# A hybrid RWKV-7, latent and stick-breaking attention layer: two issuing queues for the DMAs, and less filler around the inverse

## The chip, the cores and the metric

The kernel runs on one core of a Trainium2 chip. The metric is the device time of one execution in microseconds (us), as the median of the runs shown. Five engines of the core work side by side and wait for each other by semaphores: TensorE (PE in the profile; its weight loads are PEld), VectorE (DVE), ScalarE (ACT), GpSimd (POOL) and SyncE (SP), which here only issues DMAs. A DMA can be issued from SyncE or from ScalarE; an issue is an instruction in the engine's own order and stands in the trace as SPq or ACTq.

## The reference

One layer over 1024 tokens of width 1024, in float32. A normalized copy of x goes through one wide projection, its columns feed three token mixers side by side, their outputs are joined, projected and added to x, and a SwiGLU network follows.

```
h = rms_norm(x, attn_norm_g) @ w_in
r, k, v, wd, ad, gd = split(token_shift(h[..., :RW_COLS], mu))
c_q, c_kv, k_rope, sb_q, sb_k, sb_v = split(h[..., RW_COLS:])
y_rw  = rwkv7_time_mix(r, k, v, wd, ad, gd, ...)      # 8 heads of 64, a scan over time:
#   sa = S @ a_t;  S = S * w_t + sa b_t^T + v_t k_t^T;  y_t = S @ r_t
y_mla = latent attention of rms_norm(c_q) @ w_uq, rms_norm(c_kv) @ w_ukv   # 4 heads, rotary, softmax
y_sb  = stick-breaking attention of sb_q, sb_k, sb_v                        # 4 heads
x = x + concat(y_rw, y_mla, y_sb) @ w_o
hn = rms_norm(x, ffn_norm_g)
x = x + (silu(hn @ w_gate) * (hn @ w_up)) @ w_down    # 2816 hidden
```

## The kernel before

**Products.** A float32 product is made of three TensorE products (`mm3`) of a high and a low part of each operand: `wsplit` copies the high part on ScalarE and subtracts on GpSimd (or another engine), so every weight takes a load, an activation and a subtraction. `load_split` loads a block of 128 columns of `w_in` (512 KB) into one of three buffers `wr` and splits it. Products go to banks of PSUM that are given out by tag ("cu", "cy", "av", "b" and others); a tag has a fixed number of buffers, and a new user waits until the last one's copy out is done.

**Stages.** First the projection of r, k, v of the RWKV heads (column blocks in pairs of heads, `pr` 0 to 3, and halves of 512 tokens), and the operands of the scan in chunks of 64 tokens. For a chunk and head these are a strictly lower triangular 64 x 64 matrix (`d_a`), the matrices in `d_ch` (Lt, BK and RX side by side, 1 MB for each of 16 chunks) and the values (`d_v`). All go to DRAM and come back in another layout. In `s3` VectorE masks a bank into the tile `gs` (two buffers), and three DMAs store parts of it: the transposed part (`lt_out`), a block of `d_rx` (the RX part of `d_ch`) and the block for `d_a`.

**The inverse.** For each of the 128 pairs of chunk and head the triangular matrix is inverted. The two 32 x 32 diagonal blocks of all pairs are loaded into `TT` by 16 DMAs, and VectorE and GpSimd build their inverses in `XB` step by step (`inverse_steps`). `inverse_out` stores the first block's transpose to `d_x1t` and both blocks to `d_rx` (16 stores), `merge_loads` loads what `merge_a` needs (`x11` from `d_x1t`, `x22` back from `d_rx`), and the off-diagonal block is made by two rounds of 32 x 32 products, `merge_a` (bank `mga`, copied to `mgr`) and `merge_b` (bank `mgb`, copied to `mgm`), each for two groups of four heads, and stored to `d_rx`.

**The chain.** Sixteen `chain_step`s follow each other over the chunks. A step's operands come by `chain_loads`, issued on ScalarE: `CT` (the chunk's 1 MB of `d_ch`) and `SU` (state and values), with two buffers each. The products are y, u, s and y again, with copies on ScalarE and a sum on VectorE between them. `y_rows` normalizes rows, and after 8 and 16 chunks `rw_finish` scales them on GpSimd, transposes them (`yt`), multiplies by the gate (`gg`) and writes the mixed rows.

**Background.** A generator (`background`) yields everything else that is ready: the latent projections (`ip_ckv`, `uq`, `ukv`), the q and k heads (`tqq`, `tqk`), the stick-breaking inputs (`ip_sk`, stored by `sb_half` as a high and a low tile `sth` and `stl`), and then the attention, heads 0 to 3 stick-breaking and 4 to 7 with softmax (scores, weights `wt` split to `wth` and `wtl`, products `av`). `fill(n)` takes from it until its pieces come to n of the kernel's own estimated us. The program places such calls between the steps of the inverse (FILL_INV), after its stores (FILL_OUT), after each merge (FILL_MG), before the chain (FILL_END) and within it (FILL).

**Order.** Written order isn't issued order: a scheduler with a timeline of its own puts each engine's instructions in a row when the kernel is built, and an engine then works through its row without passing anything. After the chain comes the output projection `wo`, then the network with `hid`, `up` and `fd`.

Of the kernel before, what the change touches and what calls it, by code (L numbers as in the profile page):

```python
# [10 lines left out]
F32 = mybir.dt.float32  # L11
# [47 lines left out]
def trunk_kernel(ctx: ExitStack, tc: tile.TileContext, a: dict, out: bass.AP):  # L59
# [22 lines left out]
    def raw(ap):  # L82
        return ap.bitcast(F32)

    LNEXP = "natural_log_exp_and_others"

    def use_ln_exp():
# [34 lines left out]
    d_v = dr.tile([2, T, RWW // 2], F32, name="d_v")  # L122
    d_pl = dr.tile([RWW, NCH], F32, name="d_pl")
    d_x1t = dr.tile([RWH * NCH, L // 2, L // 2], F32, name="d_x1t")
    d_bv = dr.tile([4, P, T], F32, name="d_bv")
    d_sg = dr.tile([2, P, T], F32, name="d_sg")
    d_sq = dr.tile([2, 2 * P, T], F32, name="d_sq")
# [57 lines left out]
    def load_split(src_ap, c, name, eng=None):  # L185
        n = src_ap.shape[1] * c
        r, h, l = wtiles(name, n)
        nc.sync.dma_start(r.rearrange("p (a b) -> p a b", b=c), src_ap)
        wsplit(r, h, l, eng)
        return h.rearrange("p (a b) -> p a b", b=c), l.rearrange("p (a b) -> p a b", b=c)  # L190

# [135 lines left out]
    def sb_half(dst, blk, nm, hf, o):  # L327

        ts_ = slice(hf * HALF, (hf + 1) * HALF)
        h, l = stg(f"sth{nm}{blk}{hf}"), stg(f"stl{nm}{blk}{hf}")  # L330
        nc.scalar.activation(h, o, AF.Copy)
        tt(nc.vector, l, o, raw(h), ALU.subtract)
        for i, t_ in enumerate((h, l)):
            nc.sync.dma_start(dst[i, blk * P : (blk + 1) * P, ts_], raw(t_))

    def sb_block(c0, dst, blk, nm):
        for hf, o in enumerate(inproj_cols(c0 + blk * P, f"{nm}{blk}")):
# [3 lines left out]
    with tc.tile_pool(name="qa", bufs=1, reuse_waits="tile") as qa:  # L341
# [139 lines left out]
        def s3(pr, hf):  # L481
# [4 lines left out]
            for q in range(2):  # L486
                c0 = hf * 8 + q * 4

                ogs = [bank(f"g{n}_{e}{q}") for e in range(2)]
                for c in range(4):  # L490
                    for e, og in enumerate(ogs):
                        rows_ = slice(e * 64, e * 64 + 64)
                        nc.tensor.matmul(og[:, c * P : (c + 1) * P], BK[rows_, q * 4 + c].rearrange("p a t -> p (a t)"),
                                         AR[rows_, q * 4 + c].rearrange("p a t -> p (a t)"), start=True, stop=True)
                for e, og in enumerate(ogs):
                    gs = qa.tile([P, 4, P], F32, tag="gs", bufs=2, name=f"gs{n}_{e}{q}")
                    tt(nc.vector, gs, og.rearrange("p (c t) -> p c t", c=4), gmask[:, None, :].to_broadcast([P, 4, P]), ALU.mult)
                    lt_out(slice(c0, c0 + 4), R2[1 - e], 2 * pr + e, gs[64:128])
                    nc.sync.dma_start(d_rx[c0 : c0 + 4, R2[e], 2 * pr + e, :].rearrange("c s t -> s c t"), gs[0:64, :, 64:128])
                    nc.sync.dma_start(d_a[2 * pr + e, c0 : c0 + 4].rearrange("c s t -> s c t"), gs[0:64, :, 0:64])  # L500

            ov = bank(f"vt{n}")
            for j in range(4):
# [127 lines left out]
    nc.gpsimd.memset(XB, 0.0)  # L631
    for b in range(2):
        for h in range(RWH):
            nc.sync.dma_start(TT[h * NCH : (h + 1) * NCH, b], d_a[h, :, b * HB : (b + 1) * HB, b * HB : (b + 1) * HB])
        nc.gpsimd.memset(XB[:, b].rearrange("p a b -> p (a b)")[:, 0 : HB * HB : HB + 1], 1.0)

    def inverse_steps(j0, j1):
# [18 lines left out]
    def inverse_out():  # L656
        X1 = TT[:, 0]
        nc.vector.tensor_copy(X1, XB[:, 0].rearrange("p a b -> p b a"))
        nc.sync.dma_start(d_x1t.rearrange("n a b -> n (a b)"), X1.rearrange("p a b -> p (a b)"))
        for b in range(2):  # L660
            r0, r1 = b * HB, (b + 1) * HB
            for h in range(RWH):
                nc.sync.dma_start(d_rx[:, xrow(h) + r0 : xrow(h) + r1, h, r0:r1], XB[h * NCH : (h + 1) * NCH, b])
# [7 lines left out]
    def hb_rows(tag, h):  # L671
        return hb[tag, h // 4][h % 4 * HB : (h % 4 + 1) * HB]

    def merge_loads():
        for h in range(RWH):
            nc.sync.dma_start(hb_rows("x11", h), d_x1t[h * NCH : (h + 1) * NCH].rearrange("n a b -> a n b"))
            nc.sync.dma_start(hb_rows("x22", h), d_rx[:, xrow(h) + HB : xrow(h) + L, h, HB:L].rearrange("n a b -> a n b"))

    def merge_a(g):

        o = bank(f"mga{g}", "cu")
        for c in range(NCH):
            for k in range(4):
                ks = slice(k * HB, (k + 1) * HB)
                nc.tensor.matmul(o[ks, c * HB : (c + 1) * HB], hb["a21", g][ks, c, :], hb["x11", g][ks, c, :], start=True, stop=True)
        nc.scalar.activation(hb["mgr", g].rearrange("p c t -> p (c t)"), o, AF.Copy)

    def merge_b(g):
        o = bank(f"mgb{g}", "av")
        for c in range(NCH):  # L690
            for k in range(4):
                ks = slice(k * HB, (k + 1) * HB)
                nc.tensor.matmul(o[ks, c * HB : (c + 1) * HB], hb["mgr", g][ks, c, :], hb["x22", g][ks, c, :], start=True, stop=True)
        nc.scalar.activation(hb["mgm", g].rearrange("p c t -> p (c t)"), o, AF.Copy)
        for h in range(4 * g, 4 * g + 4):
            nc.scalar.dma_start(d_rx[:, xrow(h) : xrow(h) + HB, h, HB:L].rearrange("n a b -> a n b"), hb_rows("mgm", h))


    uqh = qb.tile([P, 2, 384], F32R, name="uqh")
# [395 lines left out]
            yield p_()  # L1095
        fin()

    FILL_INV, FILL_OUT, FILL_MG, FILL_END, FILL = 6, 34, 4, 18, 1.9
    LATE_PER_ATT = 1
    SB_POOL, MLA_POOL = (1, 3, 5), (1, 3, 5)  # L1100

# [6 lines left out]
    for h in range(RWH):  # L1108
        nc.sync.dma_start(hb_rows("a21", h), d_a[h, :, 0:HB, HB:L].rearrange("c s t -> s c t"))
    inverse_out()  # L1110
    merge_loads()
    fill(FILL_OUT)
    for g in range(2):
        merge_a(g)
        fill(FILL_MG)
    for g in range(2):
        merge_b(g)
        fill(FILL_MG)
    fill(FILL_END)
    qi_cm.__exit__(None, None, None)  # L1120

# [535 lines left out]
```

## Time and profile before

| what | value |
|---|---|
| time, median of 3 runs | 1446.31 us (1444.57 to 1447.97) |
| profiled execution, time | 1447.62 us |
| profiled execution, span | 1445.4 us |
| TensorE busy | 1341.4 us, 93% |
| VectorE busy | 921.7 us, 64% |
| GpSimd busy | 689.1 us, 48% |
| ScalarE busy | 652.5 us, 45% |
| DMA | 201.29 MB, mean 139 GB/s |

Busy times are those of one profiled execution and don't add up, since the engines work side by side. The idle share of the engine that is busiest says how much a better order could bring at all (104 us of TensorE here, over all stages), but where it stands idle, and for whom, has to be read from single stretches. The profile gives the clock that TensorE was granted in tenths of full speed; it is 9 or more in all of the 40 slices but two, at about 397 to 470 us, with 8.

### The profile page before, as it was taken

The page shows a single profiled execution, that of the slowest core. Times are in us where ns is not written, and L with a number is a line of the kernel's source. Part 1 is how long each engine was busy: PE and PEld are TensorE (multiplying, and loading weights), DVE is VectorE, ACT ScalarE, POOL GpSimd, SP SyncE. Part 2 cuts the span into 40 slices and gives each one's busy share as a digit, 9 for nine tenths or more (in the row PEclk, how much of TensorE's full clock was granted, in tenths as well). Part 3 has the DMA queues.
Part 4 walks back from the last instruction along what each step waited for, and adds up shares of the span by engine and source line. Part 5 has one row for each costly group of instructions (what it writes and reads, how often), then busy time and mean ns, then how long its engine had stood idle before and what let it go on. Part 6 is the DMA issues. An engine that isn't in the chain of part 4 may idle for free.

```text
span 1445.4 us, 21569 instructions
## 1 busy us (share of the span) xinstructions
PE 1341.4 (93%) x7717; PEld 1100.2 (76%) x7717; DVE 921.7 (64%) x1316; ACT 652.5 (45%) x1306; POOL 689.1 (48%) x664
## 2 busy tenths in 40 slices
PE   6999999898868988997998899999999999999998
PEld 6777778777656776886787688888888888778786
DVE  6566575377248899675137966656655565797755
ACT  6645345223447786886424433333333333434342
POOL 3233342376243335231605776666666666445443
PEclk9999999999988999999999999999999999999999
DMA  7226555785779652742432432322333217843242
GB/s 228 50 63 160 141 144 146 193 142 111 193 207 268 179 172 66 227 136 88 157 134 90 133 113 102 109 93 98 109 110 110 80 60 274 329 160 102 80 139 73
DMA packets 229444, 201.29 MB, mean 139 GB/s; under 512 B 92077, under 2 KB 180442, under 8 KB 227418
## 3 DMA queue, kind: packets, MB, share of 16 engines
q1 hardware_dynamic: 216362, 175.28, 41.0%
q10 hardware_dynamic: 12976, 24.65, 5.5%
q8 instruction: 61, 1.00, 0.3%
q14 instruction: 45, 0.37, 0.1%
HBM read 131.95 MB, written 67.93 MB: 138 GB/s over the span
## 4 chain that ended last, share of the span: by engine, by line
PE 58%; DVE 14%; DMA 7%; ACT 6%; SPq 5%; issue 5%; POOL 3%; ACTq 0%; DVEq 0%; POOLq 0%
PE fd L205 4%; PE fd L206 3%; PE fd L204 3%; PE wo L205 2%; PE wo L206 2%; PE wo L204 2%; PE wt L916 1%; DVE C L987 1%; PE y L1155 1%; DMA d_a<-gs 1%; DVE l_w L91 1%; DVE gs L91 1%; SPq L447 1%; DVE wd L91 1%; POOL XB L91 1%
## 5 line engine op out<-in xcount | busy, mean ns | idle before, releaser
L91 POOL TENSOR_TENSOR l_h<-hr,h_h 128x512 fp32r<-128x512 f32 x77 | 106.7, 1387 | 108.5 <-ACT h_h L1315 100.8
L205 PE MATMUL fd<-l_w,h_h 128*128 128x512 f32 x308 | 120.0, 394 | 8.9 <-DVE l_w L91 8.8
L91 DVE TENSOR_TENSOR l_w<-wd,h_w 128x512 fp32r<-128x512 f32 x77 | 90.3, 1181 | 49.4 <-ACT h_w L1315 49.3
L206 PE MATMUL fd<-h_w,l_h 128*128 128x512 f32 x308 | 118.9, 391 | 0.0
L1315 ACT ACTIVATE h_h<-hr 128x512 fp32r<-128x512 f32 x77 | 48.7, 633 | 136.3 <-PE fd L205 89.4
L204 PE MATMUL fd<-h_w,h_h 128*128 128x512 f32 x308 | 84.1, 392 | 0.0
L91 POOL TENSOR_TENSOR l_ffn_w_up<-rffn_w_up,h_ffn_w_up 128x512 fp32r<-128x512 f32 x33 | 47.1, 1428 | 67.0 <-ACT h_ffn_w_up L1315 61.3
L205 PEld LDWEIGHTS fd<-l_w,h_h 128*128 128x128 f32 x308 | 58.1, 189 | 24.0 <-DVE l_w L91 12.1
L204 PEld LDWEIGHTS fd<-h_w,h_h 128*128 128x128 f32 x308 | 58.4, 190 | 12.2
L206 PEld LDWEIGHTS fd<-h_w,l_h 128*128 128x128 f32 x308 | 58.1, 189 | 11.9
L91 POOL TENSOR_TENSOR hid<-hid,up 128x512 f32<-128x512 f32 x44 | 62.7, 1425 | 9.2 <-DVE up L91 9.2
L91 POOL TENSOR_TENSOR BD<-BK,plt 64x512 f32<-64x512 f32 (+1 forms) x24 | 35.9, 1497 | 55.1 <-DVE BK L91 41.8
L91 DVE TENSOR_TENSOR wtl<-wt,wth 128x512 fp32r<-128x512 f32 (+2 forms) x112 | 54.2, 491 | 12.3 <-ACT wth L921 8.2
L91 POOL TENSOR_TENSOR l_ffn_w_gate<-rffn_w_gate,h_ffn_w_gate 128x512 fp32r<-128x512 f32 x33 | 48.0, 1457 | 22.8 <-ACT h_ffn_w_gate L1315 22.8
L921 ACT ACTIVATE wth<-wt 128x512 fp32r<-128x512 f32 (+2 forms) x112 | 48.1, 445 | 16.8 <-PE wt L916 6.1
L1496 ACT ACTIVATE hid<-hid 128x512 f32<-128x512 f32 x44 | 27.7, 632 | 61.1 <-DVE hid L91 61.1
L205 PE MATMUL wo<-wol,mix 128*128 128x512 f32 x128 | 50.3, 394 | 0.0
L206 PE MATMUL wo<-woh,mix 128*128 128x512 f32 x128 | 50.2, 393 | 0.0
L204 PE MATMUL wo<-woh,mix 128*128 128x512 f32 x128 | 49.7, 397 | 0.0
L1315 ACT ACTIVATE h_ffn_w_gate<-rffn_w_gate 128x512 fp32r<-128x512 f32 x33 | 20.8, 631 | 61.2 <-PE P4up L205 21.5
L1315 ACT ACTIVATE h_w<-wd 128x512 fp32r<-128x512 f32 x77 | 47.5, 617 | 0.5 <-PE fd L206 0.4
L91 DVE TENSOR_TENSOR gs<-g,gmask 128x512 f32<-128x512 f32 x32 | 21.3, 684 | 38.8 <-DMA d_a<-gs 38.8
(569 smaller groups left out, 4409.1 us busy)
## 6 DMA issues: line engine op xcount, KB each, us to landing
CT<-d_ch ACTq DMA_DIRECT2D x15, 1024.0 KB
hr<-d_h SPq DMA_DIRECT2D x14, 1024.0 KB
rffn_w_gate<-in_ffn_w_gate_dram SPq DMA_DIRECT2D x11, 1024.0 KB
rffn_w_up<-in_ffn_w_up_dram SPq DMA_DIRECT2D x11, 1024.0 KB
d_h<-up SPq DMA_DIRECT2D x44, 256.0 KB
d_h<-hid SPq DMA_DIRECT2D x33, 256.0 KB
wd<-in_ffn_w_down_dram SPq DMA_DIRECT2D x8, 1024.0 KB
hr<-d_h SPq DMA_DIRECT2D x7, 768.0 KB
```

What stands on the lines that cost most here:

```text
L91: eng.tensor_tensor(o, x, y, op=op)
L204: nc.tensor.matmul(o, lh, rh, start=first, stop=False)
L205: nc.tensor.matmul(o, lh, rl, start=False, stop=False)
L206: nc.tensor.matmul(o, ll, rh, start=False, stop=last)
L447: nc.sync.dma_start(d_lt[chunks, rows, h, o].rearrange("c s t -> s c t"), src[:, :, i])
L916: nc.tensor.transpose(o[:, (sb * 2 + i) * P : (sb * 2 + i + 1) * P], W[i][:, (2 * g + sb) * P : (2 * g + sb + 1) * P], ident)
L921: nc.scalar.activation(wh[:, lo:hi], o[:, lo:hi], AF.Copy)
L987: nc.vector.tensor_tensor_scan(C[:, k1 - 1 : last : -1], st[:, k1 - 1 : last : -1], zero_c.to_broadcast([P, k1 - k0]), 1.0 if k1 == n else ...
L1155: nc.tensor.matmul(yo[:, ps[h]], Lt[:, h, :], S[:, ps[h]], start=h == 0, stop=True, skip_group_check=True)
L1315: nc.scalar.activation(hv, src, AF.Copy)
L1496: nc.scalar.activation(hid[f][hf], hid[f][hf], AF.Silu)
```

## The change

The constants for the filler become smaller (34 to 12, 4 to 2, 18 to 10), and FILL_MG is taken once between the merges instead of four times. `QUEUES` is a pair of SyncE and ScalarE. ScalarE issues the loads of `load_split`, the low tiles of `sb_half`, half of the 16 loads of the diagonal blocks, and half of the merged stores; the `d_a` store goes ahead of the two others of its tile, for the last pair of heads on ScalarE. The inverse's second block gets a DRAM buffer of its own (`d_x22`), stored by ScalarE, and the loads of `x11` and `x22` are issued before the 16 stores to `d_rx`, the former on SyncE, the latter on ScalarE. The merges' banks get a tag each in turn. No arithmetic is changed.

```diff
+    QUEUES = (nc.sync, nc.scalar)
...
+    d_x22 = dr.tile([RWH * NCH, L // 2, L // 2], F32, name="d_x22")
...
     def load_split(src_ap, c, name, eng=None):
         n = src_ap.shape[1] * c
         r, h, l = wtiles(name, n)
-        nc.sync.dma_start(r.rearrange("p (a b) -> p a b", b=c), src_ap)
+        nc.scalar.dma_start(r.rearrange("p (a b) -> p a b", b=c), src_ap)
...
         for i, t_ in enumerate((h, l)):
-            nc.sync.dma_start(dst[i, blk * P : (blk + 1) * P, ts_], raw(t_))
+            QUEUES[i].dma_start(dst[i, blk * P : (blk + 1) * P, ts_], raw(t_))
...
+                    QUEUES[pr == 3].dma_start(d_a[2 * pr + e, c0 : c0 + 4].rearrange("c s t -> s c t"), gs[0:64, :, 0:64])
                     lt_out(slice(c0, c0 + 4), R2[1 - e], 2 * pr + e, gs[64:128])
                     nc.sync.dma_start(d_rx[c0 : c0 + 4, R2[e], 2 * pr + e, :].rearrange("c s t -> s c t"), gs[0:64, :, 64:128])
-                    nc.sync.dma_start(d_a[2 * pr + e, c0 : c0 + 4].rearrange("c s t -> s c t"), gs[0:64, :, 0:64])
...
-            nc.sync.dma_start(TT[h * NCH : (h + 1) * NCH, b], d_a[h, :, b * HB : (b + 1) * HB, b * HB : (b + 1) * HB])
+            QUEUES[h % 2].dma_start(TT[h * NCH : (h + 1) * NCH, b], d_a[h, :, b * HB : (b + 1) * HB, b * HB : (b + 1) * HB])
...
         nc.vector.tensor_copy(X1, XB[:, 0].rearrange("p a b -> p b a"))
+        nc.scalar.dma_start(d_x22.rearrange("n a b -> n (a b)"), XB[:, 1].rearrange("p a b -> p (a b)"))
         nc.sync.dma_start(d_x1t.rearrange("n a b -> n (a b)"), X1.rearrange("p a b -> p (a b)"))
+        for h in range(RWH):
+            for i, (tag, d_) in enumerate((("x11", d_x1t), ("x22", d_x22))):
+                QUEUES[i].dma_start(hb_rows(tag, h), d_[h * NCH : (h + 1) * NCH].rearrange("n a b -> a n b"))
...
-    def merge_loads():
-        for h in range(RWH):
-            nc.sync.dma_start(hb_rows("x11", h), d_x1t[h * NCH : (h + 1) * NCH].rearrange("n a b -> a n b"))
-            nc.sync.dma_start(hb_rows("x22", h), d_rx[:, xrow(h) + HB : xrow(h) + L, h, HB:L].rearrange("n a b -> a n b"))
...
-        o = bank(f"mga{g}", "cu")
+        o = bank(f"mga{g}", ("cu", "cy")[g])
...
-        o = bank(f"mgb{g}", "av")
+        o = bank(f"mgb{g}", ("av", "cu")[g])
...
-            nc.scalar.dma_start(d_rx[:, xrow(h) : xrow(h) + HB, h, HB:L].rearrange("n a b -> a n b"), hb_rows("mgm", h))
+            QUEUES[h % 2].dma_start(d_rx[:, xrow(h) : xrow(h) + HB, h, HB:L].rearrange("n a b -> a n b"), hb_rows("mgm", h))
...
-    FILL_INV, FILL_OUT, FILL_MG, FILL_END, FILL = 6, 34, 4, 18, 1.9
+    FILL_INV, FILL_OUT, FILL_MG, FILL_END, FILL = 6, 12, 2, 10, 1.9
...
     inverse_out()
-    merge_loads()
     fill(FILL_OUT)
     for g in range(2):
         merge_a(g)
-        fill(FILL_MG)
+    fill(FILL_MG)
     for g in range(2):
         merge_b(g)
-        fill(FILL_MG)
     fill(FILL_END)
```

The scheduler puts the engines' rows together anew, so more moves than the diff names. Three places follow, each of before and then of after; after's line numbers are one to three higher for the same code, or lower by one behind `merge_loads`.

SyncE right after the inverse, before; `d_sq` and `d_sk` hold the stick-breaking q and k, `d_ch<-XB` are the 16 stores of the inverse, `x` the tiles x11 and x22:

```order
L334 DMA d_sq<-sthsq_3148 128x512
L334 DMA d_sq<-stlsq_3149 128x512
L1044 DMA sqk_4117<-d_sk 64x1024 x2
L663 DMA d_ch<-XB 16x32x32 x2
L659 DMA d_x1t<-TT 128x1024
L663 DMA d_ch<-XB 16x32x32 x14
L676 DMA x_2687<-d_x1t 32x16x32
L677 DMA x_2689<-d_ch 32x16x32
```

The same place on SyncE after, with `d_mq` the finished q heads:

```order
L1045 DMA sqk_4315<-d_sk 64x1024 x2
L669 DMA d_ch<-XB 16x32x32
L662 DMA d_x1t<-TT 128x1024
L669 DMA d_ch<-XB 16x32x32 x6
L665 DMA x_2688<-d_x1t 32x16x32 x4
L665 DMA x_2689<-d_x1t 32x16x32 x4
L669 DMA d_ch<-XB 16x32x32 x9
L336 DMA d_sk<-sthsk_3337 128x512
L774 DMA d_mq<-tqq_3315 96x4x256
```

The eight loads of x11 now stand behind seven of the stores and ahead of nine; before, all 16 loads stood behind all 16 stores. The eight loads of x22 have left SyncE.

TensorE around the chain's first product (`y<-SU,CT`), before; `ukv` is the last latent projection and `tqk` the transposes of k heads:

```order
L204 MATMUL ukv_3888<-ukvh,ct0ckv 128x512
L205 MATMUL ukv_3888<-ukvl,ct0ckv 128x512
L206 MATMUL ukv_3888<-ukvh,ct1ckv 128x512
L1155 MATMUL y_4636<-SU_4629,CT_4628 128x64 x8
L768 MATMUL tqk_3989<-ident,Kt_3817 96x128 x4
L768 MATMUL tqk_4001<-ident,Kt_3817 96x128 x4
L1169 MATMUL u_4715<-u0s_4645,CT_4628 64x64 x8
L768 MATMUL tqk_4010<-ident,Kt_3877 96x128 x4
```

And after, where `ip_ckv` is the projection whose result `ukv` needs:

```order
L769 MATMUL tqq_3765<-ident,Q_3343 96x128 x4
L206 MATMUL ip_ckv_3752<-xT_107,wh_ckv 128x512
L207 MATMUL ip_ckv_3752<-xT_109,wh_ckv 128x512
L208 MATMUL ip_ckv_3752<-xT_107,wl_ckv 128x512
...
L1154 MATMUL y_3794<-SU_3787,CT_3786 128x64 x8
...
L1168 MATMUL u_3836<-u0s_3803,CT_3786 64x64 x8
L769 MATMUL tqq_3823<-ident,Q_3687 96x128 x4
```

The chain begins within the `ip_ckv` projection, ahead of all of `ukv`; before, it began behind it. Before the first product of an attention head TensorE's row now holds chain steps 0 to 3 and the first product of step 4; before, it held the first two products of step 0.

TensorE behind the last attention product (`av7_3`), before; `yt1` are the transposes of the second half of the chain's rows:

```order
L941 MATMUL av7_3_7293<-wtl7_30_7341,vt7_6599 128x256
L1240 MATMUL yt10_7474<-ident_71,yn4_6401 128x128
L1240 MATMUL yt10_7474<-ident_71,yn5_6782 128x128
L1240 MATMUL yt10_7474<-ident_71,yn6_7163 128x128
L1240 MATMUL yt10_7474<-ident_71,yn7_7407 128x128
```

And after, where `wo00` is the first block of the output projection:

```order
L942 MATMUL av7_3_7532<-wtl7_30_7556,vt7_6990 128x256
L206 MATMUL wo00_7637<-woh00_7206,mix000_4549 128x512
L207 MATMUL wo00_7637<-wol00_7207,mix000_4549 128x512
L208 MATMUL wo00_7637<-woh00_7206,mix010_4550 128x512
L206 MATMUL wo00_7637<-woh01_7210,mix000_4549 128x512
```

All of `yt1` and `gg1` has gone into heads 6 and 7, and the chain's last product into head 5; the output projection follows the last head.

## Rows read from the trace of the kernel before

**Rows 1.** Windows: stretch, us, busy us of each engine, clock, DMA share, GB/s.

```profile
347.00:435.00 88.00, 66.75 (x807) 54.88 (x805) 32.75 (x47) 36.73 (x76) 33.74 (x69) 0.86 0.74 187
...
434.00:470.00 36.00, 30.49 (x262) 25.14 (x260) 29.28 (x48) 26.73 (x65) 12.92 (x23) 0.81 0.96 267
...
435.00:580.00 145.00, 126.95 (x1074) 103.59 (x1072) 130.02 (x238) 109.30 (x275) 60.36 (x85) 0.91 0.60 171
580.00:660.00 80.00, 78.46 (x730) 66.64 (x730) 56.96 (x168) 65.15 (x177) 21.12 (x26) 0.98 0.58 177
660.00:688.00 28.00, 20.37 (x131) 14.73 (x129) 15.31 (x42) 17.41 (x40) 7.95 (x8) 0.88 0.19 65
```

**Rows 2.** Waits of PE, 340 to 470 us: waiter, releaser, total us, count, longest.

```profile
PE y L1155 <- DMA CT<-d_ch: 9.0, 1, 9.0
PE mga L685 <- ACT mgr L686: 4.2, 1, 4.2
```

**Rows 3.** Timeline of SyncE, 340 to 470: start, duration, line, what, count.

```profile
346.41 0.37 SPq L659 DMA_DIRECT2D d_x1t<-TT  x1
346.83 9.88 SPq L663 DMA_DIRECT2D d_ch<-XB  x14
...
365.09 0.49 SPq L677 DMA_DIRECT2D x<-d_ch  x1
```

**Rows 4.** Timeline of PE, 340 to 430; in brackets the idle time before.

```profile
347.11 0.39 PE L206 MATMUL ip_sk<-xT,wl_sk 128*128 128x512 f32 x1
...
364.58 0.43 PE L685 MATMUL mga<-x,a 32*32 32x32 f32 x26
...
401.00 1.29 PE L693 MATMUL mgb<-x,mgr 32*32 32x32 f32 x128
...
421.27 3.65 PE L1155 MATMUL y<-SU,CT 128*128 128x64 f32 x16 [9.00 <-DMA CT<-d_ch]
```

**Rows 5.** Timeline of ScalarE, 400 to 460.

```profile
407.15 0.31 ACTq L696 DMA_DIRECT2D d_ch<-mgm  x1
...
411.64 1.19 ACTq L1137 DMA_DIRECT2D CT<-d_ch  x1
...
435.58 0.28 ACT L983 ACTIVATE st<-z 128x128 f32<-128x128 f32 x1
...
454.70 0.28 ACT L921 ACTIVATE wth<-wt 128x128 fp32r<-128x128 f32 x1 [4.05 <-DMA d_sg<-gdl]
```

**Rows 6.** Chain of waits, 655 to 720: start, duration, what.

```profile
677.39 4.05 POOL yn L91 x4
...
688.14 0.50 PE gg L204
```

**Rows 7.** Timeline of all engines, 27 to 30.

```profile
27.41 1.06 ACT L182 ACTIVATE wh_r<-wr_r 128x1024 fp32r<-128x1024 f32 x1 [3.88 <-DMA wr_r<-in_w_in_dram]
...
29.00 0.39 PE L204 MATMUL ip_wdad<-xT,h_wdad 128*128 128x256 f32 x1 [2.25 <-ACT xT L169]
```

**Rows 8.** Timeline of all engines, 284 to 300.

```profile
284.66 10.76 SPq L634 DMA_DIRECT2D TT<-d_a  x16
...
299.12 0.26 DVE L91 TENSOR_TENSOR TM<-TT,XB 128x54 f32<-128x54 f32 x1 [6.95 <-DMA d_sk<-stlsk]
```

**Rows 9.** Waits of PE, 260 to 350.

```profile
PE ip_sk L204 <- DVE stlsq L91: 5.2, 1, 5.2
```

**Rows 10.** Groups of PE, 421 to 666: count, busy us, mean ns, idle before.

```profile
L1155 PE MATMUL y<-SU,CT 128*128 128x64 f32 x256 | 34.7, 294 | 10.7 <-DMA CT<-d_ch 9.0 <-ACT yn L1199 1.7
L1180 PE MATMUL y<-SU,CT 64*64 64x64 f32 x256 | 18.0, 231 | 0.3 <-ACT SU L1171 0.2
L1169 PE MATMUL u<-u0s,CT 64*64 64x64 f32 x256 | 13.0, 239 | 0.7 <-ACT u0s L1158 0.6
L1176 PE MATMUL s<-SU,CT 128*64 128x64 f32 x240 | 11.4, 230 | 0.1
```

**Rows 11.** DMA issues, page part 6: count, KB each.

```profile
CT<-d_ch ACTq DMA_DIRECT2D x15, 1024.0 KB
```

## The prediction

> **What bounds the kernel now.** I began with the page's table of engines (it is in the section on the profile): TensorE is busy for 93% of the span, so only the stretches where it is not are worth a look. The windows view finds them [rows 1]. From 347 to 435 us TensorE works 66.75 of 88 us, at a mean granted clock of 0.86; from 435 to 580 it works 126.95 of 145 while VectorE works 130.02, so there VectorE is the nearest limit; from 580 to 660 TensorE is full (78.46 of 80); from 660 to 688 it works 20.37 of 28. After 688 us (output projection and FFN) nothing in the change reaches the work.
>
> The list of waits says what the first stretch waits for [rows 2]: 9.0 us for the first chunk's operands (CT) and 4.2 for the copy out of the first merge's bank. SyncE's timeline shows why the merge is late [rows 3]: after the inverse's last step the queue issues the transposed half at 346.41, then 14 stores one behind the other (9.88 us, 0.71 each), and only then the 16 loads that the merge needs, the last at 365.09. TensorE's timeline [rows 4]: the merge's first product starts at 364.58, its second stage ends at 402.29, and the chain over the 16 chunks starts at 421.27, 75 us behind the inverse. ScalarE's [rows 5]: the last merged store at 407.15, the chunk's load at 411.64, the first attention weights at 435.58. So the chain runs inside the attention, and its end is the tail [rows 6]: at 677.39 GpSimd scales the last rows of the chain, and the last gate product is at 688.14, with the output projection behind it.
>
> **The change part by part.** Sums are made against the profiled execution, 1447.62 us with a span of 1445.4; it stands 1.3 us above the median of the runs, 1446.31.
>
> *Weights on ScalarE's queue.* Nineteen 512 KB loads leave SyncE. At the start ScalarE waits 3.88 us for the r weights, and TensorE 2.25 us behind it [rows 7]; the load stood behind x's blocks and the small vectors in SyncE's queue, now it goes out among ScalarE's first steps. Gain between 0 and 3.9 us; I take 2, near TensorE's own wait. The price is the issue itself, 0.31 to 1.19 us of ScalarE each [rows 5]. About 48 issues more come to 15 to 57 us, spread over 345 us in which TensorE, not ScalarE, is at the limit; I take 0 on the path. A weight load also waits until GpSimd is done with the buffer, now with ScalarE's evictions queued behind it; the price of that is between 0 and, at one 3.88 us wait [rows 7] for each of three column blocks, 12 us. I take 0, since the order sets each load a few activations behind the split that it waits for.
>
> *Loads of the diagonal blocks.* Sixteen of them take 10.76 us on one queue and the inverse's first step follows at 299.12 [rows 8]. Half of them on each queue saves 5.4 us, and the stores that they read leave from ScalarE's queue ahead of other stores. So the inverse begins and ends 5 to 8 us earlier, at about 338 to 340. TensorE runs background products then; its own gain is part of the 5.2 us that it waits in the sk projection [rows 9], bounds 0 and 5.2. I take 4 for it, and it is spent at once on the wait for the merge's loads.
>
> *Halves read back first.* In SyncE's new order one store, the transposed half, 6 stores and then 8 loads follow the inverse, 9 stores behind; the x22 loads go on ScalarE. So the last load is issued 0.4 + 6 x 0.71 + 8 x 0.49 = 8.6 us behind the transposed half instead of 18.7 [rows 3]. With a few us to land, the first merge starts around 350 instead of 364.58.
>
> *Banks and filler.* The second merge_a waited for the first's bank to be copied out (4.2 us, [rows 2]); with a bank of its own it follows at once. The filler count around the merge falls from 68 to 24 of the kernel's estimated us. In TensorE's new order 21 projection products (12 of uq, 9 of sk) stand between merge_a and merge_b; at the 0.39 us of one such product [rows 4] these are 8.2 us, with the merges' own 1.3 and 1.3 the second one ends near 362. From there to the first chain product it took 421.27 - 402.29 = 19 us [rows 4]; with the same path the chain starts near 381 (370 to 390), some 40 us earlier than before.
>
> *What that is worth.* No work goes away, so the gain is idle time. In the stretch to the first attention weights (435.58) 21.3 us of idle go [rows 1]. The new order puts 3.4 chain steps there, which came later before. All chain products last 34.7 + 18.0 + 13.0 + 11.4 = 77.1 us for 16 steps, 4.8 a step [rows 10], so 16.3 us. For the wait at the first chain product I keep 5 of its 9.0 us, and 5 more for steps that stand back to back (each hands a sum to VectorE and two copies to ScalarE). A clock of 0.86 means that about a quarter of the stretch ran at 1.2 GHz instead of 2.4; fewer gaps give back 4 us, between 0 and 9. Together: 16.3 + 10 - 21.3 - 4, and 4 from the earlier arrival: -3 us (bounds +10 and -14).
>
> The attention (435 to 688) loses those 3.4 steps. While VectorE limits it (to 580), two steps fewer are worth little: I take 2 us, and 4 for ScalarE's stall of 4.05 us at 454.70, where it had issued a load into a tile that a gate store still held [rows 5]; in the new order the gate's tiles are long free when the chain asks. That is -6 (0 to -10). While TensorE limits it, 1.5 steps fewer give -7 (-3 to -10). The tail from 677.39 to 688.5 goes, for the second group of chain rows is now finished among the last heads and the projection follows the last head: -11 (-7 to -13), and nothing covers what is then last, the head's own softmax.
>
> Sum: -2 - 3 - 6 - 7 - 11 = -29. For waits that the trace of before cannot show (ScalarE held by loads, chunks landing late) I give back 5: -24, so 1423.6 in the profiled execution and 1422.3 by the median. I say 1423.
>
> **A rule against it.** The row: the chunk's load takes from 411.64 to 421.27 in a stretch that moves 187 GB/s with the DMA engines 0.74 busy [rows 1, 5]. The Trainium skill says (DMA: Bandwidth & Descriptors, Issuing engines are not separate DMA queues) that transfers started from several engines share the same 16 DMA engines, and that a second issuer saves only the issuing time. By that rule only the issue terms would stand, and the waits for data would not shrink; it is the first rival's mechanism, and whether the trace agrees is seen in the wait for CT.
>
> **Rivals.** *The transfers bind (slower).* Four more chunks of 1 MB [rows 11] move into a stretch that moves 187 GB/s x 88 us = 16.5 MB, 25% more, for a DMA share of 0.92. If each of the first five chunks then lands as late as the first did, TensorE, which works in order, stands 5 x 9.0 = 45 us where I counted 5: 1423 + 40 = 1463. For it speak the 9.0 us, and the stretch from 434 to 470, where chunks and the first heads already load side by side at 267 GB/s and a share of 0.96, with TensorE at work for 30.49 of 36 us [rows 1]; against it that each chunk has two buffers and that a step with its background products lasts some 10 us. It turns the sign once the five waits come to 24 us more than I counted, 5 a chunk.
> *The gain stays before the attention.* If VectorE, 90% busy from 435 to 580, and ScalarE set the pace to the end, the earlier chain only lengthens the idle time of TensorE among the heads: of the sum the start, half of the tail and little else stay, -2 - 6 = -8, 1438. For it speaks that no engine but TensorE is taken off work; against it the full TensorE from 580 to 660.
> *The order does not come true.* If the loads on ScalarE hold its evictions, TensorE's projections stall by as much as the chain gains, with 12 us at the start and as much around the inverse: 1446, no change.
> *More comes back.* If all idle time before 435 goes, 11 us more: 1412, inside the forecast.
>
> **How the numbers follow.** The forecast (1405 to 1434) gets 0.58, below it 0.04; the gain that stays before the attention 0.17 (1434 to 1443); no change 0.08; the transfers, or ScalarE held beyond the gain, 0.13. What a measurement can tell from no change here is 0.2%, 2.9 us. So faster 0.79, same 0.08, slower 0.13. The range leaves out 0.04 below and most of the slower case: 1404 to 1450; the likeliest case alone holds 1405 to 1434.
>
> **What would show it.** Right: the merge's products start near 350 and the chain's first near 381; the wait for CT is below 5 us; the last gate products stand before the last head's and the projection starts 20 to 30 us earlier than 688; VectorE's busy time is unchanged. Wrong: several waits of TensorE for CT or SU between 370 and 430; ScalarE idle behind DMA issues before 260 with TensorE waiting for its evictions; a start of the attention later than 440; a tail as long as before behind other work.

## The result, and the profile after

The changed kernel takes 1470.43 us (median of 4 runs, 1467.45 to 1473.11) against 1447.14 for the kernel before: a ratio of 1.016, 95% interval 1.0136 to 1.0184. It is slower by 23 us; forecast was 24 us faster. Each execution read below is one profile: 1447.62 us before (span 1445.4), 1469.94 after (span 1467.9).

**Where the 22.5 us of span went.** The views of single tiles give first and last starts of TensorE's products on them. Before (scores `z` of the stick-breaking heads, last head product `av`, output projection `wo`):

```profile
L979 PE MATMUL z<-sqk,sqk x48: 220/414/793, 433.4 to 546.7; 128*128 128x512 f32 x24, 128*128 128x128 f32 x8, 128*128 128x256 f32 x8, 128*128 128x384 f32 x8
...
L941 PE MATMUL av<-wtl,vt x96: 274/283/561, 460.8 to 677.4; 128*128 128x256 f32 x96
...
L204 PE MATMUL wo<-woh,mix x128: 389/392/477, 688.9 to 782.5; 128*128 128x512 f32 x128
```

And after:

```profile
L980 PE MATMUL z<-sqk,sqk x48: 219/458/775, 455.1 to 574.8; 128*128 128x512 f32 x24, 128*128 128x128 f32 x8, 128*128 128x256 f32 x8, 128*128 128x384 f32 x8
...
L942 PE MATMUL av<-wtl,vt x96: 274/284/467, 480.3 to 714.2; 128*128 128x256 f32 x96
...
L206 PE MATMUL wo<-woh,mix x128: 389/392/477, 714.3 to 807.6; 128*128 128x512 f32 x128
```

The transposed half of the inverse is stored at 349.39 us instead of 346.41 [rows 3], the first score comes at 455.1 instead of 433.4, the heads last 259.1 us instead of 244.0, the tail behind them is gone (0.1 instead of 11.5), and the rest, to the end of the span, is 2.9 shorter. So: 3.0 at the start, 18.7 ahead of the heads, 15.1 in them, -11.4 in the tail, -2.9 behind: 22.5. From the first score to the projection the kernel takes 259.2 us instead of 255.5, though only 12 chain steps lie there now instead of 15.

**The start.** ScalarE's timeline of after (start, duration, instruction, idle time before):

```profile
13.61 0.20 ACT L150 ACTIVATION_READ_ACCUMULATOR jk<-xin 128x1 f32 x1
19.39 0.43 ACTq L190 DMA_DIRECT2D wr_r<-in_w_in_dram  x1
19.87 0.60 ACT L171 ACTIVATE xT<-ptr 128x512 fp32r<-128x512 f32 x1 [6.07 <-DMA rows<-in_rw_k_k_dram]
```

The load of the r weights stands on ScalarE between two steps of the normalization and goes out at 19.39 only. The copy of `xT` behind it, which TensorE's first projection needs, comes at 19.87; before, it was at 13.71:

```profile
13.71 0.59 ACT L169 ACTIVATE xT<-ptr 128x512 fp32r<-128x512 f32 x1
```

The bracket in after's last row names what held it: the landing of `in_rw_k_k`, a small load of SyncE. SyncE's own small loads wait in the same way, for blocks of x (12 to 20 us; waiter, releaser, total us, count, longest):

```profile
SPq L250 <- DMA xin<-in_x_dram: 5.1, 5, 1.1
```

In the trace a DMA reports its landing to a counter (a semaphore). Eight counters are given out in turn to the DMAs of both queues, 85 or 86 times each, and an issue waits until the DMA that had its counter last, eight places before, has landed. ScalarE's load shares a counter with `in_rw_k_k`, issued on SyncE at 13.87: its last count came at 19.31, and ScalarE's wait ended at 19.33.

**The merge.** SyncE's timeline of after, with the 8 loads of x11 in the third row:

```profile
349.39 0.33 SPq L662 DMA_DIRECT2D d_x1t<-TT  x1
349.77 5.65 SPq L669 DMA_DIRECT2D d_ch<-XB  x6
355.46 6.15 SPq L665 DMA_DIRECT2D x<-d_x1t  x8
```

ScalarE's, with the 8 loads of x22 beside them:

```profile
348.29 0.35 ACTq L661 DMA_DIRECT2D d_x<-XB  x1
...
352.68 6.58 ACTq L665 DMA_DIRECT2D x<-d_x  x8
```

And TensorE's, from its last product before the merge:

```profile
350.72 0.39 PE L208 MATMUL ip_sk<-xT,wl_sk 128*128 128x512 f32 x1
359.43 0.28 PE L686 MATMUL mga<-x,a 32*32 32x32 f32 x2 [8.32 <-DMA x<-d_x1t]
...
368.28 0.32 PE L686 MATMUL mga<-x,a 32*32 32x32 f32 x14 [2.80 <-issue]
...
380.05 0.70 PE L694 MATMUL mgb<-x,mgr 32*32 32x32 f32 x58 [1.98 <-issue]
...
393.49 1.97 PE L1154 MATMUL y<-SU,CT 128*128 128x64 f32 x16 [1.49 <-DMA CT<-d_ch]
```

The merge does come earlier than in [rows 4] (359.43 for 364.58), and the chain by 28 us (393.49 for 421.27). From the transposed half to the first merge product it is 10.0 us instead of 18.2. But TensorE has nothing in hand ahead of the merge: it stands 8.3 us for the first load, and 13 us in all to the end of the first merge products. SyncE's stores and loads also follow each other more slowly than in [rows 3] (5.65 / 6 = 0.94 us for 0.71 a store, 0.77 for 0.49 a load).

**The heads.** Windows of after: the merge, the way to the first score, the stick-breaking heads, the softmax heads as far as the chain's last gate product, and what is left of them (columns as in [rows 1]):

```profile
347.00:369.00 22.00, 9.00 (x269) 7.51 (x269) 6.66 (x11) 5.56 (x12) 6.22 (x12) 0.77 0.96 175
369.00:455.10 86.10, 72.55 (x763) 61.32 (x762) 32.93 (x49) 41.84 (x91) 33.21 (x64) 0.88 0.75 214
455.10:579.30 124.20, 104.51 (x809) 84.11 (x807) 108.65 (x179) 87.87 (x215) 49.18 (x75) 0.89 0.59 170
579.30:668.60 89.30, 81.98 (x760) 69.02 (x758) 67.95 (x196) 71.91 (x191) 27.96 (x33) 1.00 0.43 132
668.60:714.30 45.70, 33.91 (x162) 27.84 (x161) 26.43 (x68) 29.77 (x71) 17.49 (x15) 0.74 0.23 78
```

The last row is new. Before, chain and gate products lay among the heads to their end and 11 us beyond. Now they end at 668.5, and for 45.7 us TensorE has nothing but the heads: it idles for 11.8 us and has a mean clock of 0.74, so about half of it at 1.2 instead of 2.4 GHz. Its longest waits there:

```profile
PE m L1003 <- ACT mw L1014: 2.1, 3, 1.0
PE wt L917 <- ACT mw L1014: 2.0, 2, 1.0
PE wt L917 <- DVE wtl L92: 1.9, 2, 1.1
```

These are the softmax's own steps, each waiting for the one before. ScalarE and GpSimd have other work in this stretch, eight of the splits of the output projection's weights (GpSimd's part: count, busy us, mean ns, idle before):

```profile
L92 POOL TENSOR_TENSOR wol<-wor,woh 128x512 fp32r<-128x512 f32 x8 | 10.0, 1271 | 9.7 <-ACT woh L184 9.7
```

All in all the softmax heads, from their first score to the projection, take 135.0 us with 6 chain steps where they took 136.0 with 8.

### The profile page after: what moved, and what is told of

Same layout as the page of the kernel before. It is cut to its first block, busy times and chain, and to the rows that moved or that the text cites. A ratio compares the mean times of both kernels' runs of the same rounds, so it can differ in the third digit from the quotient of the medians.

```text
span 1467.9 us, 21553 instructions
## 1 busy us (share of the span) xinstructions
PE 1350.0 (92%) x7717; PEld 1111.9 (76%) x7717; DVE 925.4 (63%) x1316; ACT 653.0 (44%) x1306; POOL 690.7 (47%) x664
## 4 chain that ended last, share of the span: by engine, by line
PE 47%; DVE 3%; issue 1%; POOL 1%; ACT 0%; DVEq 0%; ACTq 0%; POOLq 0%
PE fd L207 4%; PE fd L208 4%; PE fd L206 4%; PE wo L208 2%; PE wo L207 2%; PE wo L206 2%; PE P7gate L206 1%; PE P3gate L206 1%; PE P7gate L208 1%; PE P7gate L207 1%; PE P3up L206 1%; PE P7up L206 1%; PE P5up L206 1%; PE P2up L206 1%; PE P6gate L207 1%
## 5 line engine op out<-in xcount | busy, mean ns | idle before, releaser
L208 PE MATMUL fd<-h_w,l_h 128*128 128x512 f32 x308 | 118.3, 389 | 0.0
L208 PEld LDWEIGHTS fd<-h_w,l_h 128*128 128x128 f32 x308 | 57.8, 188 | 11.8
L92 POOL TENSOR_TENSOR l_ffn_w_gate<-rffn_w_gate,h_ffn_w_gate 128x512 fp32r<-128x512 f32 x33 | 48.0, 1456 | 20.5 <-ACT h_ffn_w_gate L1314 20.5
L92 DVE TENSOR_TENSOR gs<-g,gmask 128x512 f32<-128x512 f32 x32 | 21.3, 683 | 41.1 <-DMA d_ch<-gs 41.0
```

Of the source, the lines that this page charges most:

```text
L92: eng.tensor_tensor(o, x, y, op=op)
L208: nc.tensor.matmul(o, ll, rh, start=False, stop=last)
```

## The experiments

Three of the changed parts stand out, so kernels were made with one or two of them. Ratios are to the kernel before, timed on the same chip, with 95% intervals. "Steps ahead" are the chain steps whose `u` product stands ahead of the first score (1 before), "bare" is the time from the last gate product's start to the output projection's (0 before), both in the profiled execution.

| kernel | filler | weight loads | us | ratio | steps ahead | bare, us |
|---|---|---|---|---|---|---|
| after | new | ScalarE | 1470.4 | 1.0160 (1.0136 to 1.0184) | 4 | 46 |
| e1 | old | ScalarE | 1452.3 | 1.0031 (1.0013 to 1.0050) | 2 | 13 |
| e3 | new | SyncE | 1457.6 | 1.0082 (1.0056 to 1.0108) | 4 | 46 |
| e5 | old | SyncE | 1439.8 | 0.9967 (0.9949 to 0.9984) | 1 | 3 |
| e6 | FILL_OUT 34 | SyncE | 1446.8 | 1.0003 (0.9984 to 1.0023) | 2 | 0 |
| e7 | FILL_END 32 | SyncE | 1453.8 | 1.0053 (1.0028 to 1.0077) | 3 | 20 |
| e2 (before) | new | SyncE | 1457.1 | 1.0071 (1.0045 to 1.0098) | 4 | 27 |
| e4 (before) | old | ScalarE | 1457.9 | 1.0051 (1.0032 to 1.0071) | 0 | 0 |
| e8 (before, read-back) | old | SyncE | 1446.1 | 0.9999 (0.9983 to 1.0016) | 1 | 0 |

**e1: the filler alone undone.**

```diff
-FILL_INV, FILL_OUT, FILL_MG, FILL_END, FILL = 6, 12, 2, 10, 1.9
+FILL_INV, FILL_OUT, FILL_MG, FILL_END, FILL = 6, 34, 4, 18, 1.9
     (and fill(FILL_MG) after each merge again)
```

> The changed kernel with the filler constants and calls of before (34; 4 four times; 18), all DMA parts kept. Theory F (the loss is the smaller filler: TensorE stands bare at the merge, and chain steps that were free among the attention heads are paid ahead of them): 1440 to 1452 us, with the merge's 8.3 us wait gone or small. Theory Q (the loss is DMA issues that hold up ScalarE and what waits for it): the filler is no matter, 1462 to 1472.

18 us come back, at the upper edge of theory F's range. But F's reason fails in a part: the merge's wait of 8 us stays (8.0, shown under e3), with the old filler.

**e2: the kernel before with the new filler.** The reverse of that edit, in the kernel before.

> The kernel before with the new filler constants and calls alone, no DMA moved. F: slower than before by most of the 23 us, 1460 to 1475. Q: within 5 us of before, 1442 to 1452.

10 us are lost in the median (1457.05), less than F said and more than Q. The profiled execution, 1464.69 us, is the longest of the ten, so its bare 27 us belong to a long one. The filler costs with or without the new queues.

**e3: weights back on SyncE, in the changed kernel.**

```diff
-        nc.scalar.dma_start(r.rearrange("p (a b) -> p a b", b=c), src_ap)
+        nc.sync.dma_start(r.rearrange("p (a b) -> p a b", b=c), src_ap)
```

> The changed kernel with the 19 weight loads back on SyncE's queue. F: only the 3 us that the start lost come back, 1465 to 1469. Q: most of the loss comes back, 1448 to 1458.

13 us come back (11 by the ratios): Q's range. TensorE's first projection starts at 14.6 us again (20.5 in after, 14.4 before). TensorE's wait for the merge's loads, in e1 and then in e3:

```profile
PE mga L686 <- DMA x<-d_x1t: 10.0, 4, 8.0
...
PE mga L686 <- DMA x<-d_x1t: 1.4, 2, 0.8
```

So this wait goes with the weight loads and not with the filler. Of the kernels that read the halves back first, those with the later weight loads on ScalarE (after, e1, e9, e11, e13, e14) all have it, 7.4 to 8.9 us at the longest; those with them on SyncE (e3, e5 to e8, e10, e12) have at most 1.2. In e3 twelve `uq` products and eight transposes, which after has behind its first merge products, stand ahead of them.

**e4: only the weights on ScalarE, in the kernel before.** The same line the other way round.

> The kernel before with only the 19 weight loads on ScalarE's queue. F: 2 to 5 us slower than before (the start), 1448 to 1452. Q: slower by most of the 23 us, 1458 to 1470.

1457.89 (ratio 1.0051), between the two ranges. Here the chain is the later one: its last gate product stands at 700.6, 13 us behind the last head's. So F and Q both hold for a part of the loss; neither was the whole.

**e5: both undone.** The edits of e1 and e3 in the changed kernel.

> The changed kernel with the filler of before and the weight loads on SyncE: what is left of the change is the read-back ahead of the stores, the banks, and the split of the inverse's loads and the sq/sk stores. If the two losses found so far (filler some 10 to 18 us, weight loads some 8 to 13) are all there is, the rest gains what the earlier merge is worth: 1438 to 1446. If the attention sets its own time whatever comes before (theory A: from the first score to the output projection it takes about 255 us however many chain steps lie in it), 1440 to 1448, with that stretch at 252 to 260 us. If the rest of the queue split costs too (Q): 1450 or more.

1439.8: 31 us less than after (28 by the ratios), about the sum of 18 and 13, and faster than before by 0.33%. What is left of the change gains 5 to 6 us.

**e6 and e7: the same 22 of filler ahead of the merge or behind it.** In e3, FILL_OUT 12 to 34; or FILL_END 10 to 32.

> The changed kernel with weights on SyncE and only FILL_OUT back at 34 (filler ahead of the merge, none added behind it). Theory M (what the smaller filler costs is TensorE standing bare while the merge's loads come, 8 to 13 us): 1443 to 1449, as good as with all of the old filler. Theory A (the cost is each chain step ahead of the attention, 2 of them here): 1449 to 1455.

> The same with the 22 of filler put behind the merge instead (FILL_OUT 12, FILL_END 32): the merge stays bare and 3 chain steps stand ahead of the attention. M: 1455 to 1460, no better than with weights on SyncE alone (1457). A: 1453 to 1457, one step less than there.

Ahead of the merge it gives back 11 us, which is M's range, and behind it 4, which is A's. But M had nothing to cover: the merge's wait was 1.4 us in e3 already (1.1 in e7, 0.5 in e6). What does go with the time is the number of steps ahead: with the weights on SyncE, 4, 3, 2 and 1 of them (e3, e7, e6, e5) come with 1457.6, 1453.8, 1446.8 and 1439.8 us, 4 to 7 us a step. From the first score to the projection the four take 258.8, 256.7, 256.1 and 250.4 us, so the heads do not get shorter by the steps that they lose. The bare time falls along with it (46, 20, 0, 3), and the filler sets all of this together, so which of it costs is argued from this row and not shown by itself.

**e8: only the read-back, the merged stores and the banks.** `inverse_out` and the merges of after in the kernel before, filler and other queues as before.

> The kernel before with only the read-back ahead of the stores (x22 from its own buffer, by ScalarE's queue), the merged stores on two queues and the banks; filler and all other queues as before. If an earlier merge is worth something by itself: 1436 to 1444. Theory A: the merge and the chain come 10 to 20 us earlier and the time stays at 1443 to 1449.

The merge starts at 355.6 and the chain at 412.3, each 9 us earlier, and the time is the same: the chain's lead is given back, as theory A says for this case.

**e9: more products in the chain.** In after, from step 5 on, the u products three times and the s products twice.

```diff
-        for h in range(RWH):
-            nc.tensor.matmul(o[...], RX[...], u0[...], start=True, stop=True)
+        for rep in range(3 if c >= 5 else 1):
+            for h in range(RWH):
+                nc.tensor.matmul(o[...], RX[...], u0[...], start=True, stop=True)
```

> The changed kernel with products repeated in the chain's steps 5 to 15, which lie in the attention: u three times and s twice, same operands and same result; 512 passes more of TensorE at about 0.05 us each, 25 us of work. Theory A (TensorE isn't the limit among the heads; chain products there fill time in which it would stand): at most 8 us longer than the changed kernel's 1470, the rest hidden. Rival W (TensorE's work there sets the time, so steps moved ahead of the attention should have shortened it): 1490 to 1497.

With 512 products more, 25 us by the estimate above, the kernel is 13 us faster than after (1457.48, ratio 1.0057, 1.0037 to 1.0077). TensorE's busy time over the whole execution rises by 7.0 us only, at a clock of 0.965 for 0.960. Rival W is out, but the order did not stay either: the scheduler counts a longer chain and spreads its steps further, so that the last gate product starts 5.5 us before the projection.

**e10: no background within the chain.** e5 with FILL 0.

> The version of e5 with no background placed within the chain's steps (FILL 0), so that all 16 steps stand ahead of the softmax heads and none among them; otherwise the same work. A: the softmax heads (first score to output projection, 131.9 us in e5 with 8 chain steps among them) still take 118 to 130 us, and the whole 1455 to 1475. W: 8 steps x 4.8 us leave them, 93 to 97 us, and the whole stays near 1440.

1513.47 us, and both theories fail in a part. Its windows: the stick-breaking heads with their chain steps, the steps and gate products that are left, the softmax heads without a chain step, and once more the last 45.7 us of these:

```profile
430.20:548.50 118.30, 103.09 (x913) 84.51 (x912) 103.35 (x175) 87.51 (x218) 50.68 (x75) 0.90 0.64 196
548.50:659.50 111.00, 71.00 (x496) 58.46 (x495) 29.41 (x54) 32.85 (x74) 32.60 (x34) 0.56 0.31 100
659.50:758.00 98.50, 85.03 (x511) 69.53 (x512) 71.08 (x221) 75.56 (x201) 18.30 (x20) 0.92 0.22 62
712.40:758.10 45.70, 38.13 (x230) 31.09 (x230) 32.69 (x101) 35.10 (x92) 8.53 (x9) 0.93 0.13 41
```

And the stick-breaking and the softmax heads of e5:

```profile
433.40:551.80 118.40, 99.26 (x866) 81.12 (x865) 105.61 (x177) 89.61 (x223) 47.33 (x74) 0.95 0.62 188
551.80:683.80 132.00, 123.19 (x1055) 103.09 (x1054) 98.80 (x273) 105.13 (x269) 43.24 (x49) 0.96 0.41 128
```

The softmax heads have no fixed time: without the steps and the 24 gate products they take 33.5 us less, and TensorE's work there falls by 38.2. The stick-breaking heads take as long as in e5 (118.3 for 118.4), and the work that was moved takes the 111.0 us behind them, at a clock of 0.56. One wait in it has another reason, the loads for the softmax heads:

```profile
PE m L1003 <- DMA mqk<-d_mk: 14.1, 1, 14.1
```

The last seven chain steps themselves take 66.4 us (561.8 to 628.2), 9.5 each with nothing beside them, where all that was moved was worth 33.5 us among the softmax heads. So the price of a chain step depends on what stands beside it.

The last row speaks against a simple reading of after's bare stretch. It has as little beside the heads, yet in the same 45.7 us TensorE does 230 products at a clock of 0.93, where after does 162 at 0.74. That the chain has ended does not alone make heads slow. In e10 no weights of the projection are split there, as they are in after; whether that, the heads' order or something else decides was not tried.

**e11 and e14: which weight loads.** In e1, two (r and v of the first block, the edit shown) or eleven (all of r, k and v, by the same line) of them back on SyncE.

```diff
-        nc.scalar.dma_start(r.rearrange(...), src_ap)
+        QUEUES[name not in ("r0", "v0")].dma_start(r.rearrange(...), src_ap)
```

> The changed kernel with the old filler and only the first two weight loads (r and v of the first block) back on SyncE, the other 17 on ScalarE. Theory S (the weights' price is the first load, whose issue held ScalarE until 19.4 us while x's transfers filled the DMA engines): 1441 to 1446, most of the way from 1452 (all on ScalarE) to 1440 (all on SyncE). Rival E (the price lies in the later loads too): 1447 to 1452.

> The changed kernel with the old filler and the 11 loads for r, k and v on SyncE, only the 8 later ones (sq, sk, cq, ckv, gd) on ScalarE. All 19 on ScalarE took 1452, 17 of them 1447.5, none 1440. If the rest of the price lies in the r, k, v loads: 1438 to 1442. If in the 8 later ones, which are issued around the inverse: 1445 to 1450.

1447.49 (1.0001, 0.9984 to 1.0018) and 1452.41 (1.0045, 1.0030 to 1.0061, above both ranges). In both the start is that of before (14.4 us). With only the 8 later loads on ScalarE the whole price is there. With them TensorE's order changes: three chain steps ahead of the first score (at 443.2 us) for one in e5 (433.4), and the merge's 8 us wait. e11 has both as well and is a little better; why is open.

**e12: the low sq and sk stores back on SyncE**, in e5.

```diff
-            QUEUES[i].dma_start(dst[i, blk * P : (blk + 1) * P, ts_], raw(t_))
+            nc.sync.dma_start(dst[i, blk * P : (blk + 1) * P, ts_], raw(t_))
```

> The version of e5 with the low tiles' stores of sq and sk back on SyncE. In the changed kernel one of them held ScalarE from 327 to 341 us, since it waits for a subtraction that stands behind the inverse's steps on VectorE. If that hold reaches TensorE: 1434 to 1438. If TensorE has enough other work there: 1438 to 1443.

1446.11 (0.9992, 0.9965 to 1.0019), above both ranges. ScalarE's hold (14.31 us in after, 9.62 in e5) costs nothing that could be seen, and what e5 gains seems to come with this split; with overlapping intervals that is not shown. What e12 adds to e8 (the split of the diagonal blocks' loads and of `d_a`'s stores) is worth nothing measurable: 1446.1 both.

**e13: useless products behind the chain's end**, in after; the order of the rest stays.

```diff
+            if "bare" in fin:      # set where the last gate product has been issued
+                ow = bank(f"warm{name}{g}", "cu")
+                for _ in range(6):
+                    nc.tensor.matmul(ow[:, 0:256], vt[:, 2 * g, :], wh[:, 0:256], start=True, stop=True)
```

> The changed kernel, order as it is, with 126 products of 128x256 without use (operands of the heads, result never read) among the head products that come behind the chain's end. In the changed kernel TensorE is busy there for 33.9 of 45.7 us (668.6 to 714.3) at a clock of 0.74. The extra work is 15 us at 0.12 us each. Theory B (the chain ended too early: TensorE stands bare behind it, waits on the heads' own softmax steps and runs at the low clock): the stretch stays at 41 to 49 us with the clock over 0.85, the whole at 1465 to 1474. Rival W (TensorE's work sets the time there): 15 us longer or more, 1483 to 1496.

The window from the last gate product to the output projection, and the groups of TensorE in it (count, busy us, mean ns, idle before):

```profile
667.10:709.80 42.70, 39.62 (x290) 35.35 (x289) 27.21 (x72) 31.02 (x74) 17.64 (x15) 1.00 0.33 107
```

```profile
L936 PE MATMUL warm<-wth,vt 128*128 128x256 f32 x126 | 19.7, 292 | 2.0 <-ACT wth L922 1.6
L917 PE MATMUL wt<-ident,mw 128*128 128x128 f32 x52 | 7.9, 274 | 0.0
```

The second group in after:

```profile
L917 PE MATMUL wt<-ident,mw 128*128 128x128 f32 x52 | 13.6, 409 | 6.2 <-ACT mw L1014 2.0 <-DVE wtl L92 1.9 <-ACT mw L1021 1.6
```

19.7 us of work more, and the stretch is 3 us shorter: the clock is 1.00 instead of 0.74, and the same 52 transposes take 274 ns for 409. The whole, 1468.45, is that of after (1.0159, 1.0133 to 1.0185). So in these 46 us TensorE's time was free: that is shown, with the order kept. And the low clock is not what makes the stretch long: at 1.00 it still takes 42.7 us.

## Why the prediction was wrong, point by point

- *Weights on ScalarE's queue: -2 forecast.* Wrong in sign. The load went out earlier, as said, but ScalarE stood 5.6 us ahead of it, with the eviction of `xT` behind; 6.1 us late at the first projection, 3.0 left at the inverse's end. A load on ScalarE was priced at 0.31 to 1.19 us, its own row, and not at what it waits for, here the landing of another queue's load. In all the weights cost 13 us by the medians (e3, and e5 against e1), 9 to 11 by the ratios.
- *Loads of the diagonal blocks: inverse 5 to 8 us earlier.* Wrong, it ends 3 later; with the start put right it ends 1.9 and 2.7 earlier (344.5 in e14, 343.7 in e11). SyncE's eight loads take 7.9 us where eight took 5.4 [rows 8], and more than half of that are waits for landings; before, none stands in SyncE's list of waits from 284 to 296 us:

```profile
286.17 7.92 SPq L636 DMA_DIRECT2D TT<-d_a  x8
...
SPq L636 <- DMA TT<-d_a: 4.4, 4, 1.4
```

  The last load goes out at 294.4 for 294.9. The rule of the Trainium skill (DMA: Bandwidth & Descriptors, Issuing engines are not separate DMA queues) that a second issuer saves only the issuing time bears here, and the trace agrees so far: the second queue did not halve the time. In the wait for CT, where the prediction looked for it, it does not show (1.5 us). e12 against e8: the split is worth nothing.
- *Halves read back first: merge at 350.* Right as a step: from the transposed half to the merge it takes 10.0 us, where some 11 were forecast (339 to 350) and 18.2 stood before. The merge comes at 359.4, 9 late, because the inverse ends 10 later than forecast. The stores and loads between took 12.2 us on SyncE, not 8.6, but the merge began before the last of them.
- *Banks, filler, chain start at 381.* The 4.2 us wait for the bank's copy is gone; the chain starts at 393.5, 12 late, 9 of them from the merge's start. That TensorE would have work while the merge's loads come was taken for granted: it stood 8.3 us. By e1 and e3 this came with the weight loads and the order of TensorE that they bring, not with the smaller filler.
- *Stretch to the first score: -3.* It is +18.7. The steps came (TensorE is busy 87.5 us from 340 to the first score for 71.5 before, 16.0 more where 16.3 were counted), and the idle time did not go: 27.6 us where 21.9 stood before. The gain of 21.3 us of idle time was the term that had no ground.
- *Attention: -13.* The step that failed most: "The attention (435 to 688) loses those 3.4 steps". It lost three and took 15 us longer; with the tail, where -24 was forecast in all, it is +3.7 (259.2 for 255.5). The price of a step was an average over a stretch in which every step had heads beside it and every head had steps. TensorE's time there was in part free, as e13 shows for the last 46 us, so a step taken out shortens nothing there, while its time is paid in full ahead of the heads. Why these 46 us take as long as they do is open (e10).
- *Tail: -11.* Right, -11.4, and no gain: the tail of gates behind the heads became a tail of heads behind the gates.
- *The wait for CT: below 5 us.* Right, 1.5. The transfers did not bind, so the slower rival as written is out. "The gain stays before the attention" named the right place (TensorE idle among the heads) but kept the gain. "The order does not come true" named ScalarE held by loads, and had it cost the gain only. 0.13 for slower was too little, since no rival asked what the moved work had been filling. Of the signs of being wrong two came: ScalarE idle at a load with TensorE behind it (19.39), and the attention later than 440 (455.1).

What stays open: how the 8 later weight loads come to cost 9 to 13 us. That they change the planned order of TensorE, with more chain steps ahead of the heads and the merge's 8 us wait, is seen; that this is the cause is only argued, and e11, which has both, costs less.

## What to carry to other kernels

Work that stands between the steps of another dependent chain has a price only together with its neighbours: in e10 chain steps and gate products worth 33.5 us among the softmax heads took 111.0 us with nothing beside them, 14.1 of it a wait for loads. Before moving such work forward, look where it comes from and ask whether what is left there gets any shorter: here three steps fewer left the way from the first score to the projection at 259.2 us for 255.5. The fastest kernel, e5, ends chain and heads within 3 us of each other; that this is what makes it fast is not shown.

A DMA on an engine that also evicts results holds everything behind it until what it waits for has come. Read in the trace what that is: here it was the landing of a load of the other queue, eight places before.

## What the runs showed that was not expected

- **An issue can wait for the other queue.** ScalarE's load at 19.39 us came 5.6 us behind its last instruction, held by the counter that it shared with SyncE's `in_rw_k_k`. In that time SyncE issued its small loads 1.27 us apart, before as after, each held by a block of x:

```profile
13.87 0.25 SPq L250 DMA_DIRECT2D rows<-in_rw_k_k_dram  x1
15.14 0.25 SPq L250 DMA_DIRECT2D rows<-in_rw_k_a_dram  x1
```

  From 18.95 on, with these blocks landed, they come 0.3 us apart. That the hold delayed the start is shown by e3 (14.6 us).
- **Useless products can cost nothing**: e13's 19.7 us, with the clock from 0.74 to 1.00 and the whole unchanged.
- **Kernels scatter by different amounts.** e2 ran from 1448.19 us (clock 0.969) to 1464.69 (0.954), while the kernel before stayed within 1441.01 to 1450.51 on the same chip, and the four runs of e10, with the lowest clock of all (0.94), lie within 2.0 us. One profile of a kernel like e2 is one draw.
